# Two more groups of expert blocks ahead of their stage, weights split earlier, and a smaller descriptor ring

## The chip, the cores and the metric

The kernel runs on one core of one Trainium2 chip. The metric is the device time of one execution in microseconds (us), the median over several runs. Times inside an execution are microseconds from the start of the span.

## The reference

Two decoder layers over 512 tokens of width 1024. Each has a mixer (layer 0: causal pooling and retention heads; layer 1: a gated linear recurrence), a layer norm, a PEER channel mixer and a second layer norm. The change lies in PEER, which both layers run alike:

```python
q = (xt @ w_q).reshape(T, 8, 2, 128)
s = einsum('thpd,hpkd->thpk', q, sub_keys)            # 8 heads x 2 halves x 128 keys
s_top, i_top = top_k(s, 16)
cand = s_top[:, :, 0, :, None] + s_top[:, :, 1, None, :]
best, pos = top_k(cand, 16)                           # 16 of 16384 experts per head
gate = softmax(best)
act = gelu(einsum('td,thkd->thk', xt, u_tab[eid]))
out = einsum('thk,thkd->td', gate * act, v_tab[eid])
```

## The kernel before, in words

Tokens stand in four blocks of 128 (tb 0 to 3). Three of them are computed densely: instead of gathering the chosen experts, the kernel multiplies the tokens with all 16384 experts, lays the gates out as a dense table that is zero where an expert was not chosen, and multiplies. The 16384 experts are 128 blocks of 128, in 32 groups of four. The tokens of tb 3 are computed by gathering rows (`gather_rounds`), and 32 tokens of tb 0 are taken out of the first product and get their dot products from gathered u rows.

- `mm1` (L745 on) is one block's first product: `stream` loads 512 KB of `peer_ut` into a `raw` buffer (5 of them), ScalarE casts it to `hi` (L169), VectorE subtracts to get `lo` (L170; 6 buffers of each), and 24 matmuls (L185 to L187) with 352 columns write PSUM, which a Gelu empties into `ge` (L754).
- `mm2` (L1096) is one block's second product with `peer_v`: 18 matmuls of 512 columns.
- `lookahead` runs `mm1` for the first NLA groups while the routing is still computed. A group's `ge` is written to DRAM (`sp`) and read back later; the last KEEP = 2 groups stay in SBUF.
- `route_topk` projects the queries in four chunks c (weights `wq`, four tiles each through `stream`; `wchunk` takes them from `self.w0` if they are there), scores them against the keys (L851), takes the top 16 on VectorE, and then makes the `choose` of heads. Tokens of tb 0 are chosen two heads at a time inside each chunk; then `choose` runs over all eight heads for tb 3, 1 and 2. For tb 1 and 2 its results are transposed on PE (L834).
- `Scatter` serves tb 0: `place` gathers eight u rows per chunk (`urow`, L741), `dots` (L105) multiplies them, four behind tb 2 and four behind tb 3 of the chunk, `weigh` makes the gates, and `add` (L127) adds them into the DRAM table `gz`, 16 indirect transfers of GpSimd's queue per head, issued behind the chunk's last row.
- `route_gates` builds the dense gates of the other tokens in eight slices of 32 tokens (one-hot comparison and product on VectorE, L900 and L901; matmuls L910 and L911), and writes each to the DRAM table `gd` from SyncE's queue (L916).
- `experts` runs over all 128 blocks in an order that mixes groups computed ahead with fresh ones. It reads `gd` and `gz` of each group into `gt` (L1030, L138) and `ge` back from `sp` (L1028), multiplies them (L1059), splits the product into `ch` and `cl`, runs `mm2`, and beside that advances `gather_rounds` (rows L968, dots L980, sums L993).

The order of tracing sets priorities; a planner lays out each engine's instructions by priority and by when they become ready. How look-ahead blocks mix with the routing is set by costs that the generators yield: they are summed, and each 2.8 of the sum starts one block.

```python
for gen in (self.route_topk(layer, xT, kT, gz), self.route_gates(layer, kT, iot, gd)):
    for cost in gen:
        credit += cost
        while credit >= 2.8:
            credit -= 2.8
            next(look, None)
for _ in look:
    pass
```

What is left of the look-ahead after both generators is traced behind the gate slices. Two more names: `tc.issue_after` queues an instruction behind another of the same engine, and `pe`'s tag `lnb` is a 4 KB buffer of the layer norm that is free during routing.

Of the kernel before, what the change touches and what calls it, by code (L numbers as in the profile page):

```python
# [9 lines left out]
F32 = mybir.dt.float32  # L10
# [10 lines left out]
P = 128  # L21
T = 512
NTB = T // P
D = 1024
# [13 lines left out]
GQ = 8  # L38
LAG = GQ + 4
NSD = TD // 32  # L40
NLA = 19
NSZ = 4
KEEP = 2
ROT = 3
RAW = 5
QS = 8
Y2 = 1.85
YC = (1.5, 3.0, 3.0, 4.0)
AHEAD = 4
TAIL = 4  # L50
# [92 lines left out]
class Kern:  # L143
# [547 lines left out]
    def peer(self, layer, xT, hs, out):  # L691
        nc, tc, io = self.nc, self.tc, self.io
        gd = self.dram.tile([NG, P, NSD - NSZ, NB, 32], F32, name="gd%d" % layer, tag="gd%d" % layer)
        sp = self.dram.tile([NLA, P, NB, TN], F32, name="sp%d" % layer, tag="sp%d" % layer)
        with tc.tile_pool(name="pe", bufs=1) as pe:
# [37 lines left out]
        return xT  # L733

    def urow(self, pool, layer, ids, j):
        if self.urows % 4 == 3:
            t = self.pe.tile([P, D], F32, name="urow3", tag="lnb")
        else:
            t = pool.tile([P, D], F32, name="urow", tag="urow", bufs=3)
        self.urows += 1  # L740
        d = self.nc.gpsimd.indirect_dma_start(out=t, out_offset=None, in_=self.io["u%d" % layer],  # L741
                                              in_offset=bass.IndirectOffsetOnAxis(ap=ids[:, j:j + 1], axis=0))
        return t, d.ins
# [12 lines left out]
    def lookahead(self, layer, xT, sp):  # L756
        for g in range(NLA):
            ge = self.pe.tile([P, NB, TN], F32, name="ge", tag="ge", bufs=3)
            for b in range(NB):
                self.mm1(layer, g * NB + b, xT, ge[:, b, :], b % 2 == 1)  # L760
                if g >= NLA - KEEP:
                    self.kept[g] = ge
# [4 lines left out]
    def route_topk(self, layer, xT, kT, gz):  # L767
        nc, tc, io = self.nc, self.tc, self.io
        with tc.tile_pool(name="rt", bufs=1) as rt, tc.tile_pool(name="rt2", bufs=2) as rt2, \
# [7 lines left out]
            wq = io["peer_w_q"][layer]  # L777
# [6 lines left out]
            def choose(tb, h0, n):  # L784
                sv = stop[:, tb, h0 * 2:(h0 + n) * 2].rearrange("p (h two) s -> p h two s", two=2)
                s0, s1 = sv[:, :, 0, :], sv[:, :, 1, :]
                iv = itop[:, tb, h0 * 2:(h0 + n) * 2].rearrange("p (h two) s -> p h two s", two=2)
                i0, i1 = iv[:, :, 0, :], iv[:, :, 1, :]
                cand = rs2.tile([P, 8, 64], F32, name="cand", tag="cand")
                at = 0  # L790
                for a, b, m in ((0, 1, 16), (1, 4, 8), (4, 8, 4), (8, 16, 1)):
                    w = b - a
                    ov = cand[:, :n, at:at + w * m].rearrange("p h (i j) -> p h i j", j=m)
                    nc.vector.tensor_tensor(ov, s0[:, :, a:b, None].broadcast_to([P, n, w, m]),
                                            s1[:, :, None, 0:m].broadcast_to([P, n, w, m]), ALU.add)
                    at += w * m
                best = rs2.tile([P, 8, 16], F32, name="best", tag="best")[:, :n]
                pos = rs2.tile([P, 8, 16], U32, name="pos", tag="pos")[:, :n]
                for h in range(n):
                    c2 = rs2.tile([P, 64], F32, name="c2", tag="c2")  # L800
                    cv = cand[:, h, :]
                    nc.vector.max(out=best[:, h, 0:8], in_=cv)
                    nc.vector.max_index(out=pos[:, h, 0:8], in_max=best[:, h, 0:8], in_values=cv)
                    nc.vector.match_replace(out=c2, in_to_replace=best[:, h, 0:8], in_values=cv, imm_value=NEG)
                    nc.vector.max(out=best[:, h, 8:16], in_=c2)
                    nc.vector.max_index(out=pos[:, h, 8:16], in_max=best[:, h, 8:16], in_values=c2)
                    yield 0.7
                if tb == 3:
                    gate = self.gate3.rearrange("p (h s) -> p h s", h=8)
                elif tb == 0:  # L810
                    gate = gz.gate[h0 // 2]
                else:
                    gate = rs2.tile([P, 8, 16], F32, name="gate", tag="gate")
                nc.vector.tensor_tensor(gate, best, best[:, :, 0:1].broadcast_to([P, n, 16]), ALU.subtract)
                nc.scalar.activation(gate, gate, AF.Exp)
                sm = rs2.tile([P, 8], F32, name="gsm", tag="gsm")[:, :n]
                nc.vector.tensor_reduce(sm, gate, AX.X, ALU.add)
                nc.vector.reciprocal(sm, sm)
                nc.vector.tensor_tensor(gate, gate, sm[:, :, None].broadcast_to([P, n, 16]), ALU.mult)
                kk = yield from self.lookup(rs2, pos, i0, i1, thr, i16)  # L820
                fl = "p h s -> p (h s)"
                if tb == 3:
                    nc.vector.scalar_tensor_tensor(self.eid, kk[0].rearrange(fl), 128.0, kk[1].rearrange(fl),
                                                   ALU.mult, ALU.add)
                    return
                if tb == 0:
                    gz.place(self, rs2, h0 // 2, kk[0].rearrange(fl), kk[1].rearrange(fl))
                    return
                tg = slice((tb - 1) * P // GW, tb * P // GW)
                ghT, glT = kT[:, tg, 2, :], kT[:, tg, 3, :]  # L830
                yield 2.8
                pt = self.psC.tile([P, 512], F32, name="pC", tag="pC")
                for i, t in enumerate((kk[0], kk[1], gate)):
                    nc.tensor.transpose(pt[:, i * P:(i + 1) * P], t.rearrange(fl), self.ident)  # L834
                px = pt[:, :3 * P].rearrange("p (i g w) -> p i g w", i=3, w=GW)
                nc.scalar.copy(kT[:, tg, 0:2, :].rearrange("p g i w -> p i g w"), px[:, 0:2])
                gs = rs2.tile([P, P // GW, GW], F32, name="gs", tag="gs")
                nc.scalar.mul(gs, px[:, 2], GS)
                nc.scalar.copy(ghT, gs)
                nc.vector.tensor_tensor(glT, gs, ghT, ALU.subtract)  # L840

            for c in range(4):
                qs = []
                keys = rt2.tile([P, 4, P], F32, name="keys", tag="keys")
                nc.sync.dma_start(out=keys, in_=io["keysT"][layer][:, c * 4:c * 4 + 4, :])
                self.proj_T(wq, c, xT, sink_q, early=c == 0)
                for tb in range(NTB):
                    ts = slice(tb * P, (tb + 1) * P)
                    ps = self.psB.tile([P, 512], F32, name="pB", tag="pB")
                    for i in range(4):  # L850
                        nc.tensor.matmul(ps[:, i * P:(i + 1) * P], qs[i][:, ts], keys[:, i, :],  # L851
                                         start=True, stop=True)
                    ixs = rs2.tile([P, 4, 16], U32, name="ix", tag="ix", bufs=2)
                    for i in range(4):
                        hp = c * 4 + i
                        sc = ps[:, i * P:(i + 1) * P]
                        mx = stop[:, tb, hp, :]
                        ix = ixs[:, i, :]
                        s2 = rs2.tile([P, P], F32, name="s2", tag="s2")
                        nc.vector.max(out=mx[:, 0:8], in_=sc)  # L860
                        nc.vector.max_index(out=ix[:, 0:8], in_max=mx[:, 0:8], in_values=sc)
                        nc.vector.match_replace(out=s2, in_to_replace=mx[:, 0:8], in_values=sc, imm_value=NEG)
                        nc.vector.max(out=mx[:, 8:16], in_=s2)
                        top = nc.vector.max_index(out=ix[:, 8:16], in_max=mx[:, 8:16], in_values=s2)
                    nc.vector.tensor_copy(itop[:, tb, c * 4:c * 4 + 4, :], ixs)
                    yield YC[c]
                    if tb == 0:
                        yield from choose(0, c * 2, 2)
                        if c:
                            gz.add(self)  # L870
                    else:
                        n = (0, 1, 1)[tb - 1] * QC // 2
                        yield 1.3 * n
                        with tc.issue_after(top.ins):
                            gz.dots(self, n)
                gz.weigh(self, rs2)
                if c == 0:
                    gz.add(self)
            gz.add(self, 8)
            for tb in (3, 1, 2):  # L880
                yield from choose(tb, 0, 8)
# [347 lines left out]
```

## Time and profile before

| what | value |
|---|---|
| median of 3 runs | 2803.01 us (2802.81 to 2809.61) |
| the profiled execution | 2803.68 us, span 2801.9 us |
| PE, VectorE (DVE), ScalarE (ACT), GpSimd (POOL) busy | 98%, 84%, 40%, 48% of the span |
| bytes moved | 788.34 MB, 281 GB/s over the span from and to HBM |
| granted TensorE clock, mean | 0.992 |

The profiled execution is 0.7 us above the median. In the rows that follow, a window's numbers are its width, the busy time of each engine in it with the instruction count, the granted clock of PE, the busy share of the 16 DMA engines and GB/s. A row of waits names who waited for whom, the sum in us, how often, and the longest. A row of the chain or the timeline begins with the start and the length of a piece. SPq, ACTq are the sequencers that issue transfers. PEld is the weight load, which overlaps PE. A matmul's recorded length overlaps the next one's; the chain's pieces give the step from one to the next.

### The profile page before, as it was taken

The page shows a single profiled execution, that of the slowest core. Times are in us where ns is not written, and L with a number is a line of the kernel's source. Part 1 is how long each engine was busy: PE and PEld are TensorE (multiplying, and loading weights), DVE is VectorE, ACT ScalarE, POOL GpSimd, SP SyncE. Part 2 cuts the span into 40 slices and gives each one's busy share as a digit, 9 for nine tenths or more (in the row PEclk, how much of TensorE's full clock was granted, in tenths as well). Part 3 has the DMA queues.
Part 4 walks back from the last instruction along what each step waited for, and adds up shares of the span by engine and source line. Part 5 has one row for each costly group of instructions (what it writes and reads, how often), then busy time and mean ns, then how long its engine had stood idle before and what let it go on. Part 6 is the DMA issues. An engine that isn't in the chain of part 4 may idle for free.

```text
span 2801.9 us, 41670 instructions
## 1 busy us (share of the span) xinstructions
PE 2745.8 (98%) x15314; PEld 2449.4 (87%) x15314; DVE 2359.3 (84%) x4556; ACT 1116.5 (40%) x1575; POOL 1352.6 (48%) x865
## 2 busy tenths in 40 slices
PE   9999999999999999999999999999989999999998
PEld 7899899988888888888788898999978888888886
DVE  6678989867898989888798677899868888988887
ACT  3353336543333333333334343445543333333332
POOL 0006667864565666553000017667764556555651
PEclk9999999999999999999999999999999999999999
DMA  6357776999999999998222557686999999999993
GB/s 228 127 178 227 236 221 178 248 270 366 382 386 382 390 377 396 374 383 295 95 83 72 203 177 203 194 245 177 277 308 361 378 398 368 389 388 382 384 383 146
DMA packets 318318, 788.34 MB, mean 281 GB/s; under 512 B 62113, under 2 KB 128161, under 8 KB 318113
## 3 DMA queue, kind: packets, MB, share of 16 engines
q1 hardware_dynamic: 175808, 410.75, 41.4%
q0 software_dynamic: 120128, 303.22, 32.0%
q10 hardware_dynamic: 22176, 71.71, 6.4%
q8 instruction: 120, 1.97, 0.3%
q14 instruction: 86, 0.70, 0.1%
HBM read 708.50 MB, written 77.07 MB: 280 GB/s over the span
## 4 chain that ended last, share of the span: by engine, by line
PE 86%; DVE 7%; DMA 3%; POOL 2%; issue 1%; ACT 1%; SPq 0%; DVEq 0%; POOLq 0%; ACTq 0%
PE pB L1096 18%; PE pC L1096 18%; PE pA L187 12%; PE pA L185 12%; PE pA L186 12%; PE pC L185 2%; PE pC L186 2%; PE pC L187 2%; POOL gz L127 2%; DMA urow<-in_u,ids 2%; DVE lo L170 1%; PE pB L910 1%; DMA gd<-gbuf 1%; PE pB L911 1%; PE pB L851 1%
## 5 line engine op out<-in xcount | busy, mean ns | idle before, releaser
L169 ACT CAST hi<-raw 128x1024 fp32r<-128x1024 f32 (+1 forms) x609 | 637.8, 1050 | 962.9 <-PE pC L1096 368.2
L170 DVE TENSOR_TENSOR lo<-raw,hi 128x1024 fp32r<-128x1024 f32 (+1 forms) x609 | 733.7, 1215 | 184.5 <-ACT hi L169 156.4
L187 PE MATMUL pA<-xThi,lo 128*128 128x352 f32 (+2 forms) x1872 | 628.7, 336 | 11.2 <-DVE lo L170 11.2
L185 PE MATMUL pA<-xThi,hi 128*128 128x352 f32 (+2 forms) x1872 | 631.2, 337 | 0.6 <-ACT hi L169 0.3
L968 POOL DMA_INDIRECT row<-in_u,eid x256 | 407.3, 1591 | 464.4 <-DVE av L980 369.2
L186 PE MATMUL pA<-xTlo,hi 128*128 128x352 f32 (+2 forms) x1872 | 627.4, 335 | 0.6 <-DVE xTlo L170 0.6
L127 POOL DMA_INDIRECT gz<-gate,idx x256 | 486.2, 1899 | 130.6 <-issue 84.2
L968 POOL DMA_INDIRECT row<-in_v,eid x256 | 361.9, 1414 | 145.1 <-issue 58.5
L187 PEld LDWEIGHTS pA<-xThi,lo 128*128 128x128 f32 x1872 | 353.7, 189 | 28.6 <-DVE lo L170 14.1
L185 PEld LDWEIGHTS pA<-xThi,hi 128*128 128x128 f32 x1872 | 354.0, 189 | 18.3 <-ACT hi L169 1.2
L186 PEld LDWEIGHTS pA<-xTlo,hi 128*128 128x128 f32 x1872 | 353.9, 189 | 17.3 <-DVE xTlo L170 1.2
L993 DVE SCALAR_TENSOR_TENSOR h<-row,cf,h 128x1024 f32<-128x1024 f32 x256 | 329.4, 1287 | 6.7 <-DMA row<-in_v,eid 6.4
L980 DVE CUSTOM_DVE_ANT_0 row<-row,x 128x1024 f32<-128x1024 f32 x256 | 311.6, 1219 | 10.0 <-DMA row<-in_u,eid 9.7
L1096 PE MATMUL pB<-hi,ch 128*128 128x512 f32 x768 | 300.2, 391 | 17.9 <-DMA raw<-in_peer_ut 9.7
L1096 PE MATMUL pC<-hi,ch 128*128 128x512 f32 x768 | 299.9, 390 | 0.0
L1096 PE MATMUL pC<-lo,ch 128*128 128x512 f32 x768 | 299.6, 390 | 0.0
L1096 PE MATMUL pB<-hi,cl 128*128 128x512 f32 x768 | 299.6, 390 | 0.0
L1096 PE MATMUL pB<-lo,ch 128*128 128x512 f32 x768 | 299.5, 390 | 0.0
L1096 PE MATMUL pC<-hi,cl 128*128 128x512 f32 x768 | 299.3, 390 | 0.0
L170 DVE TENSOR_TENSOR cl<-gt,ch 128x768 fp32r<-128x768 f32 x128 | 122.0, 953 | 117.0 <-ACT ch L169 117.0
L741 POOL DMA_INDIRECT urow<-in_u,ids x64 | 86.9, 1358 | 273.4 <-ACT ids L87 203.7
L169 ACT CAST ch<-gt 128x768 fp32r<-128x768 f32 x128 | 107.2, 837 | 249.4 <-PE pC L1096 152.2
(280 smaller groups left out, 4541.9 us busy)
## 6 DMA issues: line engine op xcount, KB each, us to landing
raw<-in_peer_ut SPq DMA_DIRECT2D x256, 512.0 KB
raw<-in_peer_v SPq DMA_DIRECT2D x256, 512.0 KB
gd<-gbuf SPq DMA_DIRECT2D x16, 2048.0 KB
gt<-gd ACTq DMA_DIRECT2D x60, 512.0 KB
sp<-ge SPq DMA_DIRECT2D x34, 704.0 KB
ge<-sp ACTq DMA_DIRECT2D x34, 704.0 KB
raw<-in_peer_w_q SPq DMA_DIRECT2D x32, 512.0 KB
gz<-zero SPq DMA_DIRECT2D x64, 256.0 KB
```

The source lines that it names most:

```text
L127: d = nc.gpsimd.indirect_dma_start(out=flat, out_offset=bass.IndirectOffsetOnAxis(ap=self.idx[c][:, j:j + 1], axis=0), in_=gate[:, j:j + 1 ...
L169: self.nc.scalar.copy(hi, src)
L170: return self.nc.vector.tensor_tensor(lo, src, hi.bitcast(F32), ALU.subtract)
L185: nc.tensor.matmul(ps, ah, bh, start=(first and i == 0), stop=False)
L186: nc.tensor.matmul(ps, ah, bl, start=False, stop=False)
L187: nc.tensor.matmul(ps, al, bh, start=False, stop=(last and i == n - 1))
L741: d = self.nc.gpsimd.indirect_dma_start(out=t, out_offset=None, in_=self.io["u%d" % layer], in_offset=bass.IndirectOffsetOnAxis(ap=ids[:, ...
L851: nc.tensor.matmul(ps[:, i * P:(i + 1) * P], qs[i][:, ts], keys[:, i, :], start=True, stop=True)
L968: nc.gpsimd.indirect_dma_start(out=t, out_offset=None, in_=io[name], in_offset=bass.IndirectOffsetOnAxis(ap=at, axis=0))
L980: dot = nc.vector.tensor_tensor_reduce(ur, ur, x, 1.0, 0.0, ALU.mult, ALU.add, av[:, k:k + 1])
L993: nc.vector.scalar_tensor_tensor(acc, vr, c, acc, ALU.mult, ALU.add)
L1096: nc.tensor.matmul(acc[hf], a[:, ts], b[:, hf * 512:(hf + 1) * 512], start=first and i == 0, stop=last and i == 2)
```

## The change

Five edits. The look-ahead has 21 groups instead of 19, so 84 blocks instead of 76. The yielded cost of a head in the eight-head `choose` of tb 3, 1 and 2 is 1.2 instead of 0.7, and of two gate steps 2 x 1.6 instead of 2 x 1.85. The next chunk's four weight tiles are streamed (loaded and split) at tb 3 of a chunk, ahead of the last four dots, instead of at the start of the next chunk. The u rows rotate through six buffers and `lnb` instead of three and `lnb`. And the ring that GpSimd's transfer descriptors are written to gets 4096 bytes per partition, where the kernel before leaves the default of 16384.

```diff
-NLA = 19
+NLA = 21
...
-Y2 = 1.85
+Y2 = 1.6
...
     def urow(self, pool, layer, ids, j):
-        if self.urows % 4 == 3:
+        if self.urows % 7 == 6:
             t = self.pe.tile([P, D], F32, name="urow3", tag="lnb")
         else:
-            t = pool.tile([P, D], F32, name="urow", tag="urow", bufs=3)
+            t = pool.tile([P, D], F32, name="urow", tag="urow", bufs=6)
...
                     nc.vector.max_index(out=pos[:, h, 8:16], in_max=best[:, h, 8:16], in_values=c2)
-                    yield 0.7
+                    yield 0.7 if tb == 0 else 1.2
...
                         n = (0, 1, 1)[tb - 1] * QC // 2
+                        if tb == 3 and c < 3:
+                            self.w0 = [self.stream(wq[c + 1, k]) for k in range(4)]
                         yield 1.3 * n
                         with tc.issue_after(top.ins):
                             gz.dots(self, n)
...
-    nc = bacc.Bacc("TRN2", target_bir_lowering=False, num_devices=1)
+    nc = bacc.Bacc("TRN2", target_bir_lowering=False, num_devices=1, dynamic_dma_scratch_size=4096)
```

## The prediction

> **What bounds the kernel now.** I read the page first, then the windows by stage, then windows around every place where PE stood still, and the chain of work back from each of them.
>
> ```profile
> PE 2745.8 (98%) x15314; PEld 2449.4 (87%) x15314; DVE 2359.3 (84%) x4556; ACT 1116.5 (40%) x1575; POOL 1352.6 (48%) x865
> PE 86%; DVE 7%; DMA 3%; POOL 2%; issue 1%; ACT 1%; SPq 0%; DVEq 0%; POOLq 0%; ACTq 0%
> ...
> core 0: us, PE busy (x) PEld busy (x) DVE busy (x) ACT busy (x) POOL busy (x), PEclk, DMA share, GB/s
> 300.00:480.00 180.00, 174.92 (x1045) 168.64 (x1044) 164.18 (x704) 85.33 (x124) 122.96 (x76) 0.98 0.71 200
> 640.00:1340.00 700.00, 699.25 (x3432) 609.39 (x3431) 613.92 (x709) 251.46 (x303) 377.16 (x249) 1.00 0.95 368
> 2085.00:2780.00 695.00, 695.00 (x3410) 606.40 (x3409) 607.04 (x696) 248.38 (x298) 375.50 (x249) 1.00 0.95 367
> ```
>
> PE is the bound nearly everywhere, and without a gap in both expert stages (640 to 1340, 2085 to 2780). The number of matmuls stays the same, so time can come only from stretches in which PE idles or runs at a reduced clock. Eight windows hold the idle stretches that the edits touch, four in each layer (columns as above):
>
> ```profile
> 222.00:228.00 6.00, 4.23 (x18) 2.88 (x17) 5.01 (x22) 1.41 (x2) 5.09 (x4) 1.00 0.87 310
> 283.00:291.00 8.00, 4.70 (x20) 3.27 (x19) 7.98 (x31) 0.00 (x0) 6.78 (x5) 1.00 0.79 245
> 450.00:480.00 30.00, 24.92 (x138) 24.18 (x137) 30.00 (x124) 15.40 (x20) 25.64 (x15) 0.89 0.66 151
> 612.00:644.00 32.00, 23.82 (x130) 20.93 (x128) 14.99 (x18) 8.86 (x14) 13.69 (x12) 0.89 0.95 344
> 1668.00:1676.00 8.00, 6.52 (x28) 4.76 (x27) 7.31 (x26) 2.00 (x3) 7.09 (x4) 1.00 0.85 288
> 1730.00:1738.00 8.00, 4.72 (x15) 3.54 (x14) 8.00 (x30) 0.00 (x0) 6.60 (x4) 0.74 0.77 251
> 1896.00:1926.00 30.00, 25.37 (x149) 24.64 (x148) 30.00 (x144) 15.45 (x20) 22.43 (x13) 0.94 0.60 152
> 2060.00:2092.00 32.00, 22.26 (x111) 19.93 (x111) 14.50 (x18) 7.97 (x12) 16.61 (x15) 0.84 0.96 337
> ```
>
> Width less PE busy is the idle time: 1.77, 3.30, 5.08, 8.18, 1.48, 3.28, 4.63 and 9.74 us, 37.5 us together. Width times (1 - PEclk) is clock withheld: 3.3, 3.5, 2.1, 1.8 and 5.1 us in the five windows below 1.00, 15.8 us. Part of that was withheld while PE had nothing to do; I count half, 7.9 us. In three kinds: behind the gate slices (612, 2060) 17.9 + 4.3 = 22.2 us; the head choice ahead of the gates (450, 1896) 9.7 + 2.6 = 12.3 us; the u rows at chunk boundaries (222, 283, 1668, 1730) 9.8 + 1.0 = 10.9 us. All of it is 45.4 us: what the edits can win at most.
>
> [...]
>
> **Part 1: two more groups ahead (NLA 21).** Eight blocks of 24 matmuls per layer leave the expert stage and run earlier. Prices, from the chain of work:
>
> ```profile
> 607.02 0.16 PE pA L186
> 613.58 9.28 DMA gd<-gbuf
> 643.15 0.23 PE pB L1096
> ...
> 2060.68 11.11 DMA gd<-gbuf
> 2072.76 8.52 DMA raw<-in_peer_ut
> 2081.29 0.80 PE pB L1096
> ```
>
> A block ahead costs 24 x 0.16 = 3.84 us, so 30.7 us leave each expert stage. They come back at the same price elsewhere, less the idle time they fill. So the move itself is worth zero, and everything depends on where the eight land. Adding up the costs that the generators yield (one block per 2.8): before 220.8 in all, so all 76 blocks are traced inside, 57 up to the end of the choice and 19 in the gate slices; after 224.8, so 80 inside, 62 and 18, and four left over. Five more blocks stand beside the choice, one fewer beside the gates, four behind them.
>
> *The four behind.* In layer 1 the last gate slice is sent at 2060.68 and the first expert matmul starts at 2081.29. In between PE has three or four fresh blocks and then 9.74 us of nothing, because the slice must land (11.11 us) and its gates be read back and multiplied. Four more blocks are 15.4 us of work that needs none of this: the hole is filled with 5.6 us to spare, in layer 0 (8.18) with 7.2. I take all 22.2 us. The condition is that the reads are not pushed back. They stand in SP's queue behind loads that wait for a free raw buffer:
>
> ```profile
> 614.40 4.82 SPq L175 DMA_DIRECT2D raw<-in_peer_v  x1
> 622.93 0.80 SPq L1030 DMA_DIRECT2D gt<-gd  x2
> 624.33 1.04 ACT L169 CAST hi<-raw 128x1024 fp32r<-128x1024 f32 x1 [2.39 <-PE pA L186]
> 630.99 0.83 ACT L169 CAST ch<-gt 128x768 fp32r<-128x768 f32 x1 [5.25 <-DVE gt L1059]
> ```
>
> If that order were kept, the load ahead of them would get its buffer 15.4 us later, and most of the hole would open again (second rival). The order is laid out by when things become ready, which speaks for the reads moving forward.
>
> **Part 2: the costs 1.2 and 1.6.** In the choice DVE is full and PE runs out:
>
> ```profile
> 435.00:456.50 21.50, 21.50 (x99) 1.00 0.62 167
> 435.00:456.50 21.50, 4.84 (x4) 1.00 0.62 167
> 470.00:480.00 10.00, 8.60 (x36) 8.44 (x37) 10.00 (x44) 2.21 (x5) 8.47 (x6) 0.66 0.60 118
> 471.45 0.20 DVE kb L954
> 471.70 0.69 PE pC L834 x2
> ```
>
> The first row is DVE in one head choice, the second the `lo` splits (L170) in it: four in 21.5 us, each worth one block, so 15.4 us of PE food per 21.5 us. PE drains its stock and at 467 stands before the transpose that needs kb. Two more blocks in each of the later choices and one in the first bring 3.84 us of PE work for 1.21 us of DVE time (4.84 over 4). Two make 7.7 us more food per choice: 23.1 for 21.5 + 2.4 = 23.9 us. Nearly balanced, not fully. I take 70%: 8.6 us. The splits themselves lengthen DVE's chain by 5 x 1.21 = 6 us per layer, under PE's 5 x 3.84 = 19 us in the same stage, so they cost nothing; without that cover they would cost 12 us in the two layers. In the gates one block fewer takes 3.84 us of PE and 1.2 us of DVE away.
>
> **Part 3: weights split early, seven row buffers, ring of 4096.**
>
> ```profile
> DVE urow L105 <- DMA urow<-in_u,ids: 17.4, 7, 6.9
> ...
> 269.18 2.01 POOL gz L127
> 271.50 8.64 DMA urow<-in_u,ids
> 280.17 1.23 DVE urow L105
> 288.67 1.14 DVE lo L170
> 289.85 0.50 PE pA L187
> ```
>
> At 280 DVE stands 6.9 us before the first dot of chunk 1. The row came late not for want of a buffer, but because POOL issued sixteen adds (L127) until 271.2 ahead of it. Seven buffers do not move that row; they only make the second four dots free of waits, and let adds start earlier. What helps is the early split: the four weight tiles are traced ahead of about two blocks (5.2 of cost), so PE has the projection ready while DVE stands. Against it: the four tiles hold four of six `hi`/`lo` buffers for two blocks longer, and a block may then wait for its split behind four dots (4 x 1.23 = 4.9 us, 1.1 us more than a block lasts), up to 6.6 us at six boundaries. Ends: +10.9 and -6.6 us; I take half of the gain, 5.4 us, since the wait at 287 to 290 is for exactly these tiles.
>
> The ring has no row of its own. From below its cost is zero: it does no work. From above: POOL is busy 377 of 700 us in the expert stage with 249 instructions, so each transfer may be 1.3 us dearer before POOL is full. At most six rows are in flight there. I take zero. [...]
>
> **Part 4: transfers in the expert stage.**
>
> ```profile
> 920.00:990.00 70.00, 70.00 (x339) 60.56 (x338) 62.86 (x74) 24.98 (x30) 39.92 (x27) 1.00 1.01 401
> SPq L175 <- DVE lo L170: 648.8, 172, 23.9
> raw<-in_peer_ut SPq DMA_DIRECT2D x256, 512.0 KB
> ge<-sp ACTq DMA_DIRECT2D x34, 704.0 KB
> ```
>
> 368 GB/s x 700 us = 257.6 MB. Eight loads go (4.2 MB), two reads come (1.4 MB): 254.8 MB in 669.3 us, 381 GB/s. 70 us at 401 GB/s passed with PE full, and SP waits for buffers (648.8 us), not for data. So zero, but the reserve shrinks from 8% to 5%.
>
> **Sum.** 22.2 + 8.6 + 5.4 = 36.2 us, less 1.5 us for small stalls that the balance in part 2 and the smaller reserve in part 4 may bring (a guess): 34.7. From 2803.7 us (span 2801.9) that is 2769; the median of the runs, 2803.0, is 0.7 lower, so 2768.
>
> **Rivals.**
> 1. *Everything closes*: 45 us, 2758. For it: the five added blocks (38 us in two layers) exceed the idle 9.7 us by far. Against: DVE stays full. 15%.
> 2. *The reads stay behind the loads.* The load ahead is issued by 619.2 + 15.4 = 634.6, the reads about 635; from reads to `ch` it was 622.9 to 631.8, 9 us, so the first expert matmul comes at 644. PE's fresh blocks end at 624.4 + 15.4 = 639.8. 4 us of hole stay per layer and 2 us of clock behind each: part 1 gives 10 us instead of 22.2, the whole 22.5, 2781. 17%.
> 3. *Slower: the expert stage becomes bound by transfers*, since more blocks need `ge` back and the rest of the work is denser. Price: if 368 GB/s is all it sustains, 254.8 MB take 692 us instead of 669, 46 us in two layers, against 34.7 won: 2814. It decides below 254.8 MB / (669.3 + 17.4 us) = 371 GB/s. The window of 401 speaks against it. 6%. [...]
> 4. *No difference*: the smaller ring holds POOL up by what the rest wins, 1.3 us per transfer and a little more. 4%.
>
> The forecast itself gets 58%: 2760 to 2779. With rivals 1 and 2 and the bounds of part 3 the range is 2752 to 2790. A measurement of this kernel tells 0.3%, 8.4 us, from no change. Faster 0.89, same 0.05, slower 0.06.
>
> **What would show it.** PE idle time behind the gates near zero with eight blocks between the last gate matmul and the first of L1096; PEclk 1.00 there. The L834 transposes start without a gap. No PE wait for `lo` at the projection's start, though DVE still waits for the first u row of chunk 1. Expert stage near 669 us at about 381 GB/s with PE full. Wrong would be: gt<-gd issued later than the landing of gd; PE waits for L169 or L170 in the expert stage; POOL instructions longer than the 1.5 us that they average in that stage now (377.16 over 249).

## The result, and the profile after

The changed kernel takes 2780.67 us (median of 4 runs, 2778.95 to 2784.32) beside 2802.91 us of the kernel before on the same chip: ratio 0.9917, 95% interval 0.9899 to 0.9936. It is faster by 22 us; the forecast was 35 us, within a range that holds the result. The profiled execution took 2778.95 us, with a span of 2777.2 us and a mean clock of 0.995.

The windows of the changed kernel, at the places that the prediction showed of before, moved to where those stretches now lie:

```profile
205.00:230.00 25.00, 23.34 (x129) 20.34 (x128) 24.36 (x108) 6.76 (x14) 10.06 (x8) 1.00 0.79 286
281.00:293.00 12.00, 4.61 (x17) 4.03 (x16) 10.18 (x36) 0.00 (x0) 10.47 (x6) 0.70 0.89 290
450.00:480.00 30.00, 30.00 (x191) 30.00 (x190) 30.00 (x89) 19.76 (x25) 25.34 (x11) 1.00 0.63 170
628.00:660.00 32.00, 32.00 (x192) 30.86 (x191) 18.23 (x22) 12.50 (x18) 15.06 (x12) 1.00 0.92 342
1640.00:1665.00 25.00, 23.36 (x129) 20.37 (x128) 24.38 (x108) 7.04 (x14) 11.89 (x8) 1.00 0.78 285
1716.00:1728.00 12.00, 3.13 (x13) 2.50 (x12) 9.77 (x33) 0.00 (x0) 10.15 (x7) 0.78 0.94 298
1896.00:1926.00 30.00, 30.00 (x193) 29.98 (x192) 29.76 (x117) 16.92 (x20) 26.95 (x11) 1.00 0.75 195
2066.00:2098.00 32.00, 32.00 (x187) 30.41 (x186) 19.62 (x26) 12.54 (x18) 16.66 (x13) 1.00 0.95 353
660.00:1320.00 660.00, 660.00 (x3200) 572.24 (x3199) 593.16 (x681) 236.14 (x283) 360.94 (x247) 1.00 0.98 385
```

Width less PE busy again. Behind the gates (628, 2066) PE never idles, where 8.18 and 9.74 us stood before. In the choice (450, 1896) it never idles either and the clock is 1.00, where 5.08 and 4.63 us stood. At the first chunk boundary (205, 1640) 1.66 and 1.64 us are idle, in several short waits, where one wait had made most of 1.77 and 1.48: nothing is won there. (The 2.6 us that an expectation below gives to chunk 0 come from narrower windows that miss some of these waits.) And at chunk 1 the holes have grown: 7.39 us (281) and 8.87 us (1716), with the clock at 0.70 and 0.78, where 3.30 and 3.28 us stood. Wider windows around chunk 1 hold all of its reduced clock; first the kernel before, then the changed one:

```profile
240.00:300.00 60.00, 56.70 (x330) 52.55 (x329) 51.00 (x214) 23.33 (x38) 46.84 (x29) 1.00 0.77 225
1680.00:1740.00 60.00, 56.73 (x319) 52.80 (x318) 48.56 (x209) 23.97 (x38) 41.58 (x26) 0.95 0.72 207
```

```profile
240.00:300.00 60.00, 52.61 (x300) 49.95 (x299) 51.14 (x214) 23.62 (x37) 50.55 (x32) 0.91 0.74 215
1680.00:1740.00 60.00, 51.13 (x300) 48.45 (x299) 48.05 (x212) 20.87 (x35) 50.55 (x32) 0.94 0.78 221
```

Before: 6.6 us idle and 3.0 us of clock withheld; after: 16.3 and 9.0 us. With half of the withheld clock, as in the prediction, that is 8.1 against 20.8 us, so chunk 1 cost 12.7 us more. The three kinds now add up: +22.2 us behind the gates, +12.3 in the choice, and at the boundaries nothing at chunk 0 and -12.7 at chunk 1. Together 21.8 us; with all of the withheld clock instead of half it is 25.6. The spans differ by 24.7, the medians by 22.2.

The hole at chunk 1 of the changed kernel in order of time (start, length, what ended the wait before it in brackets): the loads that SyncE issues, then VectorE's instructions, then PE's.

```profile
244.09 3.04 SPq L175 DMA_DIRECT2D raw<-in_peer_w_q  x3
253.14 0.33 SPq L175 DMA_DIRECT2D raw<-in_peer_w_q  x1
266.02 2.75 SPq L175 DMA_DIRECT2D raw<-in_peer_ut  x2
```

```profile
271.82 1.19 DVE L170 TENSOR_TENSOR lo<-raw,hi 128x1024 fp32r<-128x1024 f32 x1
...
277.12 1.22 DVE L105 CUSTOM_DVE_ANT_0 urow<-urow,xx 128x1024 f32<-128x1024 f32 x1 [2.92 <-DMA urow<-in_u,ids]
...
286.33 1.21 DVE L170 TENSOR_TENSOR lo<-raw,hi 128x1024 fp32r<-128x1024 f32 x1
...
288.65 1.21 DVE L170 TENSOR_TENSOR lo<-raw,hi 128x1024 fp32r<-128x1024 f32 x1
```

```profile
278.69 0.40 PE L185 MATMUL pA<-xThi,hi 128*128 128x512 f32 x1
...
282.13 0.39 PE L185 MATMUL pA<-xThi,hi 128*128 128x512 f32 x1
289.91 0.66 PE L187 MATMUL pC<-xThi,lo 128*128 128x352 f32 x1 [7.39 <-DVE lo L170]
```

PE starts the projection (512 columns) at 278.69 and gets through 16 matmuls. Then, in its fixed order, comes a matmul of a look-ahead block (352 columns) that needs a `lo`. VectorE makes no `lo` between 273.0 and 286.3, because the four dots, which wait for rows, are ahead of it in its own order. PE resumes 0.05 us after the second one ends (289.86).

Loads and splits are equal in number (614) and go in the same order, and with five `raw` buffers a load goes out when the split five places ahead of it has ended (the one at 266.02 behind the split of 264.76, which ends at 265.95). Counted so, the splits at 267.18, 269.50 and 271.82 are of the first three weight tiles, the one at 286.33 is of the fourth, and the one at 288.65 is of the block loaded at 266.02, which PE waits for. So only three of the four tiles are split ahead of the dots. The same place in the kernel before, VectorE and then PE:

```profile
270.89 1.19 DVE L170 TENSOR_TENSOR lo<-raw,hi 128x1024 fp32r<-128x1024 f32 x1
286.27 1.20 DVE L170 TENSOR_TENSOR lo<-raw,hi 128x1024 fp32r<-128x1024 f32 x1
```

```profile
287.53 0.50 PE L187 MATMUL pA<-xThi,lo 128*128 128x512 f32 x1 [2.63 <-DVE lo L170]
```

VectorE made no `lo` for 14.2 us here before the change too (272.1 to 286.3), so the stretch is not new. Before, two blocks and two weight tiles were split ahead of the dots and the other two tiles behind them; now it is one block and three tiles, and the fourth tile and the next block follow. One block has changed places with a tile. PE ran dry at 284.90 and went on behind the first split (287.53); now it runs dry at 282.52 and waits for the second (289.91). In layer 1 the order of loads and splits has changed in the same way.

### The profile page after: what moved, and what is told of

It reads as the page before. It is cut to its first block, busy times and chain, and to the rows that moved or that the text cites. A ratio compares the mean times of both kernels' runs of the same rounds, so it can differ in the third digit from the quotient of the medians.

```text
span 2777.2 us, 41653 instructions
## 1 busy us (share of the span) xinstructions
PE 2737.9 (99%) x15314; PEld 2442.7 (88%) x15314; DVE 2357.1 (85%) x4556; ACT 1115.8 (40%) x1575; POOL 1344.2 (48%) x865
## 4 chain that ended last, share of the span: by engine, by line
PE 85%; issue 7%; DVE 3%; POOL 3%; DMA 2%; ACT 0%; SPq 0%; DVEq 0%; POOLq 0%; ACTq 0%
PE pC L1098 19%; PE pB L1098 19%; PE pA L187 11%; PE pA L185 11%; PE pA L186 11%; PE pC L185 3%; PE pC L187 3%; PE pC L186 3%; POOL gz L127 2%; DMA urow<-in_u,ids 1%; PE pB L912 1%; PE pB L913 1%; PE pB L851 1%; DVE oh L902 1%; POOL urow L741 1%
## 5 line engine op out<-in xcount | busy, mean ns | idle before, releaser
L185 PE MATMUL pA<-xThi,hi 128*128 128x352 f32 (+2 forms) x1808 | 606.7, 336 | 1.9 <-ACT hi L169 1.4
L187 PE MATMUL pA<-xThi,lo 128*128 128x352 f32 (+2 forms) x1808 | 604.3, 334 | 0.9 <-DVE lo L170 0.9
L186 PE MATMUL pA<-xTlo,hi 128*128 128x352 f32 (+2 forms) x1808 | 604.1, 334 | 0.8 <-DVE xTlo L170 0.8
L127 POOL DMA_INDIRECT gz<-gate,idx x256 | 494.2, 1930 | 132.4 <-issue 79.9
L970 POOL DMA_INDIRECT row<-in_v,eid x256 | 356.2, 1391 | 145.0 <-DVE h L995 66.8
L185 PEld LDWEIGHTS pA<-xThi,hi 128*128 128x128 f32 x1808 | 339.7, 188 | 19.2 <-ACT hi L169 2.5
L186 PEld LDWEIGHTS pA<-xTlo,hi 128*128 128x128 f32 x1808 | 339.6, 188 | 16.7 <-DVE xTlo L170 1.2
L187 PEld LDWEIGHTS pA<-xThi,lo 128*128 128x128 f32 x1808 | 339.5, 188 | 16.5 <-DVE lo L170 2.2
L187 PE MATMUL pC<-xThi,lo 128*128 128x352 f32 x672 | 218.6, 325 | 17.4 <-DVE lo L170 17.3
L185 PE MATMUL pC<-xThi,hi 128*128 128x352 f32 x672 | 220.4, 328 | 0.1
```

The costliest lines, as they stand in the source:

```text
L127: d = nc.gpsimd.indirect_dma_start(out=flat, out_offset=bass.IndirectOffsetOnAxis(ap=self.idx[c][:, j:j + 1], axis=0), in_=gate[:, j:j + 1 ...
L185: nc.tensor.matmul(ps, ah, bh, start=(first and i == 0), stop=False)
L186: nc.tensor.matmul(ps, ah, bl, start=False, stop=False)
L187: nc.tensor.matmul(ps, al, bh, start=False, stop=(last and i == n - 1))
L970: nc.gpsimd.indirect_dma_start(out=t, out_offset=None, in_=io[name], in_offset=bass.IndirectOffsetOnAxis(ap=at, axis=0))
```

## Experiments

Each edit is against the kernel named; what was measured is a median with its ratio to the kernel before on the same chip, whose medians were 2803.6 to 2804.4 us.

**The early split left out.** The changed kernel without its two lines:

```diff
-                        if tb == 3 and c < 3:
-                            self.w0 = [self.stream(wq[c + 1, k]) for k in range(4)]
```

> The changed kernel without the early split of the next chunk's weights; seven row buffers, the small ring, 21 groups and the new costs stay. Theory A (order): the four weight tiles, traced ahead of two look-ahead blocks, put those blocks' lo splits behind the four dots of chunk 1, and PE's fixed order has such a block inside the projection, so PE idles 7.4 and 8.9 us where it idled 3.3 before. Then the two holes at chunk 1 shrink to about 3.3 us each (9.7 us less), about 2 us of withheld clock go with them, and 2.6 us return at chunk 0: 2780.7 - 9.1 = about 2771.5. Theory B (rows): seven rows fetched at once land later each, and that holds DVE; then the holes stay and only chunk 0's 2.6 us return: 2783. Theory C (the new costs put other blocks at this place): holes stay, 2781 to 2783.

Measured: 2769.14 us, ratio 0.9875 (0.9859 to 0.9890); the profiled execution took 2776.11 us. Chunk 1 is back near what it was before the change:

```profile
240.00:300.00 60.00, 57.38 (x327) 53.15 (x326) 48.91 (x210) 23.39 (x34) 50.52 (x32) 0.97 0.76 218
1680.00:1740.00 60.00, 55.65 (x308) 51.34 (x307) 46.47 (x211) 19.39 (x33) 50.55 (x32) 0.94 0.73 213
```

2.62 and 4.35 us are idle instead of 7.39 and 8.87, and the kernel is 11.5 us faster than with the early split. The early split is a loss.

**Only the groups and the costs.** The kernel before with NLA 21, Y2 1.6 and the yield of 1.2:

> The kernel before with 21 groups and the new costs alone; row buffers, ring and the place of the weight splits as before. Theory A: it wins the holes behind the gates (22.2 us) and in the choice (12.3 us) and keeps the old ones at the chunk boundaries: 2802.9 - 34.5 = 2768.4. Theory B: the same. Theory C: the holes at chunk 1 are as large as in the changed kernel, 7 to 9 us, and it ends at about 2780.

Measured: 2768.23 us, 0.9874 (0.9859 to 0.9889). Against the run above it lacks the seven buffers and the ring, and differs by 0.9 us: these two are worth nothing that can be measured.

**Only the early split.** The two lines in the kernel before:

> The kernel before with the early split of the weights alone. Theory A: the holes at chunk 1 grow from 3.3 us to 7 to 9 us, those of chunk 0 shrink by 2.6 us in all: 2802.9 + 9 = 2812, slower than before. Theories B and C: at chunk 1 the early weights help or do nothing: 2795 to 2803.

Measured: 2816.67 us, 1.0047 (1.0034 to 1.0061), 13 us slower than before. The hole at chunk 1 is 7.81 us in layer 0 (281 to 293) and 7.95 us in layer 1, where it lies later:

```profile
1736.00:1748.00 12.00, 4.05 (x15) 3.55 (x14) 11.34 (x38) 0.00 (x0) 8.87 (x6) 0.68 0.82 289
```

So the loss doesn't depend on the other edits.

**All dots of chunk 1 behind tb 3.** The changed kernel, early split included, with the dots later and thus most of the rows landed by then:

```diff
-                        n = (0, 1, 1)[tb - 1] * QC // 2
+                        n = ((0, 0, 2) if c == 1 else (0, 1, 1))[tb - 1] * QC // 2
```

> The changed kernel with all eight dots of chunk 1 behind tb 3 (none behind tb 2), so that they come some 16 us later, when the rows have landed. Theory A: DVE no longer stands before the first row, the splits are not held, and PE's holes at chunk 1 (16.3 us and about 3 us of clock) shrink to what eight dots in a row (9.8 us of DVE) leave, 0 to 4 us each: 2762 to 2771. If the rows are not what DVE waits for at heart (theory C), nothing changes: 2781.

Measured: 2769.47 us, 0.9881 (0.9866 to 0.9896). 

```profile
240.00:300.00 60.00, 58.84 (x338) 54.35 (x337) 51.20 (x214) 24.79 (x39) 46.18 (x30) 1.00 0.75 220
1680.00:1740.00 60.00, 58.84 (x336) 54.16 (x335) 50.10 (x207) 24.78 (x39) 48.27 (x31) 1.00 0.73 218
```

1.16 us are idle in each layer, at full clock. The large holes at chunk 1 need dots that wait ahead of the look-ahead's `lo`.

**Both cures.** The dots later and no early split:

> The version without the early split, with all eight dots of chunk 1 behind tb 3. The holes that were left at chunk 1 (2.6 us in layer 0, 3.7 + 0.6 us in layer 1, and the clock behind the longer one) go, those at chunk 0 (2.7 and 1.2 us) stay: 2769.1 - 7 to 8 = about 2762. If eight dots in a row hold the splits as long as the late row did: 2769.

Measured: 2760.18 us, 0.9843 (0.9829 to 0.9856), the fastest kernel of this study, 20 us below the changed one.

```profile
240.00:300.00 60.00, 60.00 (x347) 55.94 (x346) 51.62 (x214) 24.64 (x39) 49.28 (x32) 1.00 0.76 217
```

PE never idles at chunk 1, in layer 1 (1680 to 1740) neither. Even where most rows have landed, the early split costs 9.3 us (2769.47 against 2760.18), little less than the 11.5 us with the dots in their old place. All of it is lost ahead of the expert stages: the first expert matmul comes 5.5 us later in layer 0 (649.5 against 644.0), and layer 1 adds 4.8. Part of it shows as single waits for a split between 213 and 454 us; the rest I did not place. So the early split is shown to be the loss, and the wait behind the dots is where most of it lies in the changed kernel; why it costs nearly as much without that wait stays open.

**Only the costs, with 19 groups.**

```diff
-Y2 = 1.85
+Y2 = 1.6
...
-                    yield 0.7
+                    yield 0.7 if tb == 0 else 1.2
```

> The kernel before with the new costs alone: 19 groups, so all 76 blocks stand earlier and none is left behind the gates. Theory (the terms of the sum are separate): the holes in the choice close (12.3 us), those behind the gates stay or grow, since no look-ahead block stands there: 2803.6 - 12.3 = 2791. Rival (the two go together: the costs only pay when more blocks exist): 2803, with the hole behind the gates grown by what the choice won.

Measured: 2803.65 us, 0.9995 (0.9986 to 1.0004), no difference; the first number failed.

```profile
440.00:480.00 40.00, 40.00 (x255) 39.98 (x254) 40.00 (x159) 25.60 (x30) 33.17 (x15) 1.00 0.64 171
610.00:640.00 30.00, 16.91 (x82) 14.82 (x80) 11.36 (x15) 6.69 (x10) 15.25 (x14) 0.72 1.04 356
2060.00:2090.00 30.00, 16.00 (x78) 14.09 (x78) 11.47 (x15) 6.29 (x9) 12.40 (x13) 0.77 1.02 348
```

The choice is filled (440, no idle time), and behind the gates 13.1 and 14.0 us stand idle, 9.2 us more than the 8.18 and 9.74 of before, with more clock withheld as well. Blocks that fill one hole are missing in the other; the second number on record, 2803, is the one that came.

**Only the groups, old costs.** NLA 21 in the kernel before, nothing else:

> The kernel before with 21 groups ahead and nothing else changed: the costs that the choice and the gate steps yield stay 0.7 and 1.85. By these costs 78 of the 84 blocks are traced inside and 6 behind the gate slices. Theory (one supply of blocks, the costs decide only where they lie): the holes behind the gates close as in the kernel with both edits, the holes inside the choice stay with their reduced clock, 8 to 12 us, so 2768.2 + 8 to 12 = 2776 to 2780. Rival (with enough blocks the costs play no part): 2768, no difference from the kernel with both.

Measured: 2783.14 us, 0.9918 (0.9904 to 0.9931), 3 us above the theory's range.

```profile
440.00:480.00 40.00, 35.77 (x213) 35.03 (x212) 40.00 (x175) 23.99 (x31) 32.00 (x20) 0.96 0.58 131
612.00:644.00 32.00, 32.00 (x194) 32.00 (x193) 8.58 (x7) 11.04 (x17) 7.83 (x8) 1.00 1.02 363
1890.00:1930.00 40.00, 34.63 (x207) 33.90 (x207) 39.90 (x150) 24.72 (x30) 30.59 (x17) 0.96 0.69 182
```

Behind the gates all is closed (612); in the choice 4.23 and 5.37 us are idle and 3.2 us of clock withheld, 11.2 us with half of the latter; by the runs it is 14.9 us against 21 groups with the new costs. The two edits side by side:

| us | old costs | new costs |
|---|---|---|
| 19 groups | 2802.9 to 2804.4 (before) | 2803.65 |
| 21 groups | 2783.14 | 2768.23 |

The groups alone bring 20 us, the costs alone nothing, and the costs on top of the groups 15.

**20 groups, new costs.** 80 blocks, none of which is left behind the gate slices:

> The kernel before with the new costs and 20 groups: 80 blocks, all traced inside the generators, none left behind the gate slices. Theory (what counts is PE work ahead of the first expert matmul, wherever it is traced): with 19 groups and these costs the holes behind the gates were 13.1 and 14.0 us; four more blocks are 15.4 us and fill them: 2803.65 - 27 - some 4 us of clock = 2772, the same as 21 groups (2768.2) within 0.3%. Rival (the four left behind are what fills the hole; blocks traced inside only stretch the stages ahead): holes of some 13 us stay, 2800.

Measured: 2777.30 us, 0.9900 (0.9886 to 0.9914).

```profile
630.00:650.00 20.00, 16.43 (x79) 13.24 (x78) 12.66 (x17) 5.25 (x7) 10.38 (x10) 1.00 1.01 395
```

3.57 us idle are left behind the gates in layer 0, of 13.1 with 19 groups and the same costs. Most of the hole is filled all the same. The prediction had the hole filled by the four blocks that are traced behind the gates; here a block that was traced earlier is the one that runs there. The time is 5 us above the 2772 expected and 9 us above that of 21 groups; this hole is a part of that.

**24 groups, new costs.** 96 blocks, 16 left behind the gates:

> The kernel before with the new costs and 24 groups: 96 blocks, 16 left behind the gate slices. No hole is left that they could fill, so nothing is won over 21 groups (2768.2). The expert stage then has 250.7 MB in about 623 us, 402 GB/s, where 21 groups showed 381 over the stage and windows up to 408. If the transfers sustain it: 2768 within 0.3%. If not (the transfer rival): PE waits for hi or lo in the expert stage; at 385 GB/s the stage takes 651 us instead of 623, 56 us in two layers: 2824.

Measured: 2809.20 us, 1.0019 (1.0008 to 1.0030), 41 us slower than with 21. A window in the expert stage and two rows of the waits in it, first with 24 groups, then the same of the changed kernel:

```profile
700.00:1300.00 600.00, 590.87 (x2775) 501.92 (x2774) 547.84 (x639) 206.97 (x246) 359.97 (x243) 0.99 1.00 399
...
ACT hi L169 <- DMA raw<-in_peer_v: 74.5, 30, 6.6
...
ACT hi L169 <- DMA raw<-in_peer_ut: 39.6, 19, 4.3
```

```profile
700.00:1300.00 600.00, 600.00 (x2921) 521.29 (x2921) 544.39 (x626) 214.51 (x258) 341.39 (x234) 1.00 0.99 390
...
ACT hi L169 <- DMA raw<-in_peer_ut: 18.0, 9, 3.5
...
ACT hi L169 <- DMA raw<-in_peer_v: 14.7, 9, 2.3
```

ScalarE waits 114 us for weights to land instead of 33, and PE idles 9.1 us in 600; what it waits for most in that window is ScalarE's `ch` (6.9 us). From the first to the last expert matmul it is 646.6 us; by 21 groups' 675.6 less 12 blocks' 46.1 us it should be 629.5; PE's idle time makes up some 10 of these 17 us, and I did not place the rest. In the holes that end at 796 and 982 us `ch` stands in ScalarE's order right behind a cast that waited 4.9 and 6.6 us for weights. In the one that ends at 880 it waits for VectorE's product `gt`, which stands behind dots that waited 2.8 us for a gathered row. So late transfers are in these holes, but so is VectorE, which is busy for 548 of the 600 us; no run separates the two, and 22 and 23 groups were not run. The rate alone does not tell the two kernels apart. The same stretch of layer 1, the changed kernel and then 24 groups:

```profile
2170.00:2700.00 530.00, 530.00 (x2568) 459.11 (x2567) 485.80 (x561) 189.52 (x227) 315.12 (x210) 1.00 1.00 397
2170.00:2700.00 530.00, 519.01 (x2442) 441.45 (x2441) 481.95 (x559) 181.15 (x214) 313.05 (x212) 0.99 1.00 398
```

At 397 GB/s PE is full, at 398 it idles 11 us. The expectation had worked out that a full PE would need 402 GB/s on average with 24 groups.

**Head 0's adds not issued behind chunk 0.** The changed kernel with its adds left to a later chunk, to let the rows of chunk 1 go ahead of them:

```diff
-                if c == 0:
-                    gz.add(self)
```

> The changed kernel without the adds of head 0 behind chunk 0; each later chunk adds one head and the last five follow at the end, so chunk 1's rows no longer stand behind sixteen adds in GpSimd's queue. If these adds are why the rows come late, DVE does not wait at chunk 1, the splits are in time, and PE's holes there (16.3 us and some 3 us of clock) go: about 2762. The adds end some 33 us later, near 650 instead of 617 in layer 0, behind which gz is read; that can open a hole of up to 15 us behind the gates in each layer: then up to 2792. If the landing itself were slow and not the queue, the holes at chunk 1 stay: 2781.

Measured: 2801.51 us, 0.9996 (0.9985 to 1.0007), a miss. Chunk 1's hole shrank (281 to 293: 3.19 us idle instead of 7.39), but the adds came out last of all. GpSimd, ScalarE and its queue, then ScalarE's one long wait:

```profile
647.30 1.54 POOL L127 DMA_INDIRECT gz<-gate,idx  x1 [0.30 <-issue]
...
650.46 0.33 ACTq L138 DMA_DIRECT2D gt<-gz  x1
650.83 1.04 ACT L169 CAST hi<-raw 128x1024 fp32r<-128x1024 f32 x1 [23.16 <-DMA gz<-gate,idx]
```

```profile
630.00:660.00 30.00, 15.03 (x83) 14.74 (x82) 4.36 (x4) 5.42 (x8) 22.54 (x18) 0.72 0.53 135
```

The last add is issued at 647.30. ScalarE's queue holds the read of `gz`, which needs it, and everything of ScalarE behind that read, the casts and Gelus of the look-ahead too, stood for 23.2 us. PE ran out and idled 15 us behind the gates.

**Only the ring.** 4096 bytes in the kernel before:

> The kernel before with the ring of 4096 bytes and nothing else. If the ring costs nothing: 2803.6 within 0.3%, and GpSimd's transfers have the mean times of the kernel before (1591, 1414 and 1899 ns). If the smaller ring holds GpSimd up: POOL's busy time and its transfers are longer, and the time rises from the point at which rows come late.

Measured: 2804.63 us, 1.0003 (0.9994 to 1.0011), nothing. GpSimd's adds with the small ring:

```profile
L127 POOL DMA_INDIRECT gz<-gate,idx x256 | 480.6, 1877 | 136.6 <-issue 83.9 <-DMA gz<-gate,idx 31.6 <-DVE gate L113 20.7
```

The mean of one indirect add is 1877 ns, and 1899 ns in the kernel before.

## Why the prediction was right or wrong

**Part 1, +22.2 us: right, for a reason that was half right.** The holes behind the gates are gone. The condition on the reads held, as SyncE's queue in the changed kernel shows:

```profile
620.41 0.38 SPq L918 DMA_DIRECT2D gd<-gbuf  x1
625.38 1.68 SPq L175 DMA_DIRECT2D raw<-in_peer_v  x1
630.39 0.80 SPq L1032 DMA_DIRECT2D gt<-gd  x2
631.30 13.41 SPq L175 DMA_DIRECT2D raw<-in_peer_v  x5
```

The reads go out 10 us after the last slice is sent, and the next five loads stand behind them. Rival 2, which has the same time as the result (2781), is thus not what happened: its mechanism is absent, and that the times agree is chance. "Four behind" was the wrong handle: with 20 groups and none behind, most of the hole was filled as well.

**Part 2, 8.6 of 12.3 us: too low, and not a term of its own.** All 12.3 us were won. The working that the food is "nearly balanced" was too cautious. And the sum treated the costs as separate from the groups; with 19 groups they bring nothing, since the blocks come out of the hole behind the gates.

**Part 3, +5.4 us: the step that failed.** By the windows it is -12.7 us, by the runs -12.4 (2780.67 against 2768.23). The prediction named the mechanism ("a block may then wait for its split behind four dots") but priced it as the dots' own 4.9 us less a block's 3.84, 1.1 us at six boundaries, and took half of the gain on the ground that the wait at 287 to 290 was for these tiles. Two things were wrong. The dots hold VectorE up with their waits for rows too: from the first dot at 277.12 to the next `lo` at 286.33 it is 9.2 us, not 4.9. And the tiles bring PE only 16 matmuls ahead of the next look-ahead block, not "the projection ready while DVE stands": only three of the four are split ahead of the dots, and the block that gave up its place is then missed. The lower end, -6.6, was therefore too high as well. The wait at 287 to 290 was indeed for weight tiles, but to move one of them ahead puts a block in its place. PE starts the projection without a wait, as forecast; the wait comes 16 matmuls later, for a block's `lo`, and is longer than before. That VectorE still waits for the row (2.92 us) was right. Seven buffers and ring at zero were right: 0.9 us for both together, and 2804.63 beside 2804.17 us for the ring alone. What the ring holds, at the one size or the other, no run shows.

**Part 4, zero: right.** 385 GB/s from 660 to 1320 with PE busy throughout, 381 had been worked out. Something like rival 3 shows three groups further on: with 24 groups PE waits in the stage, at 398 to 399 GB/s and with more waits for weights. Its own price, a stage that sustains no more than 368 GB/s, is refuted by 385 to 397 with PE full. GpSimd's instructions average 1.46 us in that stage (360.94 over 247), below the 1.5 named.

**The sum.** 22.2 + 12.3 - 12.7 = 21.8 in place of 34.7: too low by 3.7 in part 2, too high by 18.1 in part 3, and the 1.5 us of guessed stalls did not appear. That the result lies within the range is in part luck: part 3 came out 6.1 us below its lower end, and part 2 and the stalls gave 5.2 us back. The time of rival 1 ("everything closes", 2758) is nearly reached, at 2760.18, but by a kernel without the early split and with the dots moved.

## What to carry to other kernels

When a step is traced earlier, don't ask only whether it is ready sooner, but what now stands behind a waiting instruction in its place: here the price was the whole wait until VectorE was free (9.2 us from the first dot to the next `lo`), not the dots' own length (4.9 us). Ask as well which piece of work gives up its place. Work that fills holes is one stock: here the edit that only distributes it was worth nothing with 19 groups and 15 us with 21. Enlarge the stock until the rows of waits for transfers, not a guess, say stop (ScalarE's were 33 us with 21 groups, 114 with 24).

## What was new about the hardware

- With head 0's adds left to a later chunk, ScalarE, which issues one read of `gz` itself, did none of its own work for 23.2 us while that read waited for the last add.
- With one core at work 385 to 399 GB/s were moved over 530 us and more (385 over 660 us and 397 over 530 in the changed kernel, 399 over 600 with 24 groups). PE was full at 397 in the changed kernel and not at 398 to 399 with 24 groups, so the rate alone doesn't say whether PE has to wait.
- After the hole of 7.39 us PE ran at about half speed for 6 us, from 289.91 to 295.94, at a granted clock of 0.50: matmuls of 352 columns were 0.29 us apart, against 0.16 behind that:

```profile
290.66 0.49 PE L186 MATMUL pC<-xTlo,hi 128*128 128x352 f32 x1
290.96 0.49 PE L187 MATMUL pC<-xThi,lo 128*128 128x352 f32 x1
...
295.94 0.33 PE L186 MATMUL pC<-xTlo,hi 128*128 128x352 f32 x1
296.11 0.32 PE L187 MATMUL pC<-xThi,lo 128*128 128x352 f32 x1
```
